# A streaming hybrid encoder step: the row factor of the conv columns is applied once, squared, and the group norm's epsilon takes over the rest

## The chip, the cores and the metric

The kernel runs on one core of one Trainium2 chip. The metric is the device time of one execution in microseconds (us). Engines are named as the profile names them: PE is TensorE (matmuls; PEld are its weight loads), DVE is VectorE, ACT is ScalarE, POOL is GpSimd, SP is SyncE, which issues most DMAs here.

## The reference

One layer works on 512 new prompt rows and 64 sample rows of width 2048, together 576 rows. Only the part around the change is shown; attention and the FFN are left out.

```python
hn = rmsnorm(x, g_norm1)              # x * R * g, with R = rsqrt(mean(x*x) + EPS), one R per row
proj = hn @ w_in                      # q, k, v for 8 heads; gb, gc, hc for 8 conv groups of 128 channels
u = gc * hc
conv = conv_w[0]*padded[:, 0:T] + conv_w[1]*padded[:, 1:T+1] + conv_w[2]*padded[:, 2:T+2]
o_conv = gb * conv
mix = concat([rmsnorm(o_attn, g_attn_out), rmsnorm(o_conv, g_conv_out)])
x = x + mix @ w_out
x = x + (silu(h2 @ w_gate) * (h2 @ w_up)) @ w_down      # h2 = rmsnorm(x, g_norm2)
```

`rmsnorm(o)` divides by `sqrt(mean(o*o) + EPS)`, with EPS = 1e-6. `u` is also an output (the last two rows are the conv state), `o_conv` is not.

## The kernel before

Activations lie transposed: channels on the 128 partitions, the 576 rows along the free dimension, in two halves of 288 (`HALVES`). Matrix products are made in fp32r with each operand split into a high and a low part, three matmuls per 128-deep step (`step`, L221 for plain products). The input is multiplied by the gain `g` only; the row factor R is left out of the matmul operands and is applied to the products. `R1` (128 x 576, the same on all partitions) holds it. `eps_r` (128 x 18), made early from the rows' mean squares by a small matmul, holds EPS * (mean(x*x) + EPS), that is EPS / R^2, with row 32b + p mod 32 at partition p, column b; the q and k norms use it.

Stages, in order: the input turned and projected; eight heads (`head`, `attend`); two conv groups by plain products (`conv_group`, STD = 2), while the last head's attention ends; six conv groups in pairs, as "units" `CU`, each a 2 x 2 block product with seven multiplications in place of eight (`conv_prepare` makes the weight operands on DVE and ACT, `conv_run` multiplies and evacuates); the attention rows' output projection, as "o" units of the same kind; the conv rows' output projection (`out_proj`); the FFN, again with seven products per block (L1582). `head_forms` is a generator that runs beside the second conv group: it norms the attention output and stores its block combinations to DRAM.

What sets the order: PE runs strictly in program order (`manual_schedule`). A `Pipeline` of generators interleaves side work with the matmuls: `pipe.tick()` once per three matmuls, and a generator's `yield n` puts its next part n ticks later. DVE, ACT, POOL and SP are ordered by a scheduler when the kernel is built, except where `manual_schedule` names them: SP during the heads and from the units on, and ACT and DVE from the last half of the second conv group to the ninth unit product (`start_mode`), where program order holds. Each engine works its queue in order.

The R factors before, for a conv group: `gc` is evacuated from PSUM times R1 (L960) and again times R1 (L961); `u` is that times `hc` straight from PSUM (L933, L935); `end_u` makes the taps (L941 on ACT, L943 twice on DVE); `gb` is evacuated times R1 (L975), multiplied by the taps (`put_o`, L950 and L952) and handed to `put_mix`, which scales, squares, splits and stores it (L549, L551). For a unit pair, `done` in `conv_run` adds a kept part (L1110) and multiplies every block by R1 (L1112): the two blocks i = 0, 1 of both columns c = 0 (`gc`) and c = 1 (`hc`) of a "u" unit, and all four blocks of a "b" unit (`gb` of two groups). `group_scale` sums the squares of `o_conv` by a matmul with ones and makes R_c = rsqrt(mean + EPS) with `rsqrt_mean` (L491 to L496); `out_proj` multiplies by R_c.

## Time and profile before

| | |
|---|---|
| time, median of 3 runs | 2362.01 us (2360.82 to 2364.43) |
| the profiled execution's own time | 2360.45 us |
| its span in the profile | 2358.7 us |
| PE busy | 2335.9 us, 99% of the span, 17551 matmuls |
| DVE busy | 1894.6 us, 80% |
| ACT busy | 1134.9 us, 48% |
| POOL busy | 300.3 us, 13% |
| mean granted TensorE clock | 0.999 |

All times inside the profile are counted from the start of the span; the profiled execution's own time is 1.75 us longer than its span. A timeline row gives start, duration, engine, line, operation, the tile written and the tiles read, and in brackets how long the engine sat idle before it and what released it. A row of a wait list gives who waited, for whom, and the total, the number and the longest of the waits. A row of a stretch ("windows") gives the busy time of each engine in it, the number of instructions, the granted TensorE clock, the DMA share and GB/s. The conv groups lie at about 396 to 485 us, the unit pairs at about 478 to 690 us.

### The profile page before, as it was taken

The page shows a single profiled execution, that of the slowest core. Times are in us where ns is not written, and L with a number is a line of the kernel's source. Part 1 is how long each engine was busy: PE and PEld are TensorE (multiplying, and loading weights), DVE is VectorE, ACT ScalarE, POOL GpSimd, SP SyncE. Part 2 cuts the span into 40 slices and gives each one's busy share as a digit, 9 for nine tenths or more (in the row PEclk, how much of TensorE's full clock was granted, in tenths as well). Part 3 has the DMA queues.
Part 4 walks back from the last instruction along what each step waited for, and adds up shares of the span by engine and source line. Part 5 has one row for each costly group of instructions (what it writes and reads, how often), then busy time and mean ns, then how long its engine had stood idle before and what let it go on. Part 6 is the DMA issues. An engine that isn't in the chain of part 4 may idle for free.

```text
span 2358.7 us, 43730 instructions
## 1 busy us (share of the span) xinstructions
PE 2335.9 (99%) x17551; PEld 2325.3 (99%) x17551; DVE 1894.6 (80%) x2828; ACT 1134.9 (48%) x1975; POOL 300.3 (13%) x401
## 2 busy tenths in 40 slices
PE   8999999999999999999999999999999999999998
PEld 8999999999999999999999999999999999999998
DVE  8666666788887899888888888888888777987896
ACT  6655555444445555444444444444444444444443
POOL 1111111422121220000000000000000002431222
PEclk9999999999999999999999999999999999999999
DMA  8565563773468555344344444444444936885554
GB/s 268 153 172 142 139 166 104 240 242 114 124 236 227 173 174 160 122 154 151 122 153 141 134 153 142 133 153 132 144 153 132 359 115 206 223 236 199 190 145 87
DMA packets 588996, 395.75 MB, mean 168 GB/s; under 512 B 100222, under 2 KB 577912, under 8 KB 588792
## 3 DMA queue, kind: packets, MB, share of 16 engines
q1 hardware_dynamic: 574968, 375.95, 51.2%
q0 software_dynamic: 8624, 16.22, 3.3%
q8 instruction: 137, 2.24, 0.4%
q10 hardware_dynamic: 5200, 0.79, 0.2%
q14 instruction: 67, 0.55, 0.1%
HBM read 301.46 MB, written 91.44 MB: 167 GB/s over the span
## 4 chain that ended last, share of the span: by engine, by line
PE 89%; DVE 5%; DMA 3%; issue 1%; ACT 1%; SPq 0%; POOL 0%; ACTq 0%; POOLq 0%; DVEq 0%
PE psy L1582 34%; PE psw L1582 17%; PE pj L221 13%; PE psx L1582 8%; PE psy L1086 6%; PE pjo L221 4%; PE psw L1086 3%; PE psx L1086 1%; DMA raw_a<-in_w_out_dram 1%; DVE whl L231 1%; PE po L794 1%; PE z L723 1%; DVE whl L1058 1%; DMA out_dram<-acc 0%; DVE x L375 0%
## 5 line engine op out<-in xcount | busy, mean ns | idle before, releaser
L1582 PE MATMUL psy<-h_s,whl 128*128 128x288 f32 x2787 | 413.5, 295 | 1.1 <-ACT part L1592 1.1
L221 PE MATMUL pj<-x,whi 128*128 128x288 f32 x1856 | 388.6, 298 | 0.2
L1582 PEld LDWEIGHTS psy<-h_s,whl 128*128 128x128 f32 x2787 | 384.8, 189 | 1.8 <-ACT part L1592 1.8
L231 DVE TENSOR_TENSOR whl<-raw_a,whl 128x1024 fp32r<-128x1024 f32 (+4 forms) x296 | 318.2, 1076 | 54.6 <-ACT whl L230 53.1
L1582 PE MATMUL psw<-t,whl 128*128 128x288 f32 x2400 | 347.0, 294 | 0.0
L1582 PEld LDWEIGHTS psw<-t,whl 128*128 128x128 f32 x2400 | 327.8, 188 | 0.0
L230 ACT CAST whl<-raw_a 128x1024 fp32r<-128x1024 f32 (+4 forms) x296 | 267.5, 906 | 113.1 <-issue 35.4
L221 PEld LDWEIGHTS pj<-x,whi 128*128 128x128 f32 x1856 | 303.6, 189 | 1.4 <-DVE x L375 0.7
L221 PE MATMUL pj<-x,wlo 128*128 128x288 f32 x928 | 274.3, 296 | 0.1
L231 DVE TENSOR_TENSOR whl<-raw_b,whl 128x1024 fp32r<-128x1024 f32 (+5 forms) x190 | 200.2, 1054 | 69.5 <-ACT whl L230 68.2
L230 ACT CAST whl<-raw_b 128x1024 fp32r<-128x1024 f32 (+5 forms) x190 | 164.9, 871 | 170.3 <-issue 73.5
L1592 ACT COPY part<-psy 128x288 f32<-128x288 f32 x242 | 96.4, 398 | 284.9 <-PE psy L1582 262.0
L1582 PE MATMUL psy<-t2t,whl 128*128 128x288 f32 x1212 | 183.0, 294 | 0.8 <-ACT part L1592 0.8
L1582 PE MATMUL psy<-b22m,whl 128*128 128x288 f32 x1212 | 183.3, 295 | 0.1
L221 PEld LDWEIGHTS pj<-x,wlo 128*128 128x128 f32 x928 | 174.7, 188 | 0.7 <-DVE wlo L442 0.3
L1582 PE MATMUL psx<-h_s,whl 128*128 128x288 f32 x1185 | 173.6, 294 | 0.0
L1582 PEld LDWEIGHTS psy<-t2t,whl 128*128 128x128 f32 x1212 | 167.8, 188 | 1.1 <-ACT part L1592 1.1
L1582 PEld LDWEIGHTS psy<-b22m,whl 128*128 128x128 f32 x1212 | 168.2, 188 | 0.4 <-ACT part L1592 0.4
L1582 PEld LDWEIGHTS psx<-h_s,whl 128*128 128x128 f32 x1185 | 162.4, 188 | 0.0
L1361 POOL DMA_DIRECT2D hid_dram<-form x3 | 2.2, 749 | 947.6 <-DVE form L231 947.6
L230 ACT CAST whl<-s 128x1024 fp32r<-128x1024 f32 (+5 forms) x81 | 72.2, 892 | 102.8 <-PE psw L1582 99.4
L1582 PE MATMUL psy<-t,whl 128*128 128x288 f32 x576 | 106.5, 294 | 0.0
(474 smaller groups left out, 4297.4 us busy)
## 6 DMA issues: line engine op xcount, KB each, us to landing
hid_dram<-form SPq DMA_DIRECT2D x147, 288.0 KB, 2.3
raw_a<-in_w_in_dram SPq DMA_DIRECT2D x41, 1024.0 KB, 5.8
raw_a<-in_w_gate_dram SPq DMA_DIRECT2D x22, 1024.0 KB, 5.7
raw_a<-in_w_up_dram SPq DMA_DIRECT2D x22, 1024.0 KB, 5.8
raw_b<-in_w_gate_dram SPq DMA_DIRECT2D x22, 1024.0 KB, 6.5
raw_b<-in_w_up_dram SPq DMA_DIRECT2D x22, 1024.0 KB, 6.6
h_s<-hid_dram SPq DMA_DIRECT2D x10, 2016.0 KB, 12.8
raw_a<-in_w_out_dram SPq DMA_DIRECT2D x16, 1024.0 KB, 6.4
```

The source lines that it names most:

```text
L221: mm(ps, w_[:, k, csl], x_, start=(k == 0 and n == 0), stop=(k == nk - 1 and n == 2))
L230: nc.scalar.copy(out=hi, in_=src)
L231: (lo_eng or nc.vector).tensor_tensor(out=lo, in0=src, in1=hi.bitcast(F32), op=ALU.subtract)
L723: mm(zb[i], a_[:, kk], b_[:, q0:TP], start=(n == 0), stop=False, skip_group_check=True)
L794: mm(po[:, i * P : 512], a_[:, i, :], b_[:, : 512 - i * P], stop=(i == 0 and n == 2), **kw)
L1058: tt(out=whl[:, 1], in0=src, in1=whl[:, 0].bitcast(F32), op=ALU.subtract)
L1086: mm(ps, whl[:, w_, j, :], x_, start=(start and j == 0 and q == 0), stop=(j == m - 1 and q == 2), skip_group_check=True)
L1361: q.dma_start(out=hid_dram[fp][2 * n - 2 : 2 * n].rearrange("f p t -> p f t"), in_=t.bitcast(F32))
L1582: mm(ps, whl[:, w_, j, :], x_, start=(start and j == 0 and q == 0), stop=(j == len(xs_) - 1 and q == 2), skip_group_check=True)
L1592: nc.scalar.copy(out=t, in_=st["y"])
```

## The change

R^2 goes onto `gc` alone, in one multiplication; `hc` and `gb` get no factor. So `u`, the taps and the conv state are what they were, and `o_conv` comes out divided by R. Its norm is the same if EPS is divided by R^2 as well, which is what `eps_r` holds for each row. `R1` is squared in place once (128 x 576), after the last head's values have been read with it. In `group_scale` the 18 columns of `eps_r` are spread on ACT, each over 32 columns of R_c, and turned in 32 x 32 blocks on DVE, so that column t of R_c holds the epsilon of row t; `rsqrt_mean` then adds this tile in place of the constant. Epsilon thus lies in R_c's own tile until R_c overwrites it.

```diff
+def rsqrt_mean(..., eps=None):
+        if eps is None: (as before)
+        else:
+            nc.vector.scalar_tensor_tensor(out=ms, in0=src, scalar=1.0 / n, in1=eps, op0=ALU.mult, op1=ALU.add)
...
 def group_scale(acc, dst, rows_of):
+        nc.scalar.copy(out=dst.rearrange("p (b c) -> p b c", c=32), in_=eps_r.unsqueeze(2).to_broadcast([P, NB, 32]))
+        nc.vector.transpose(out=dst, in_=dst)
...
-            rsqrt_mean(dst[:, a:b], ss, 8 * P, HALF, ms, t)
+            rsqrt_mean(dst[:, a:b], ss, 8 * P, HALF, ms, t, eps=dst[:, a:b])
...
-    def put_o(g, i, t):
+    def put_o(g, i, src, t):
-        nc.vector.tensor_tensor(out=t[:, : e - a], in0=t[:, : e - a], in1=c[:, a:e], op=ALU.mult)
+        nc.vector.tensor_tensor(out=t[:, : e - a], in0=src[:, : e - a], in1=c[:, a:e], op=ALU.mult)
...
         def evac_gc(ps, a, b):
             nc.vector.tensor_tensor(out=t, in0=ps, in1=R1[:, a:b], op=ALU.mult)
-            nc.vector.tensor_tensor(out=t, in0=t, in1=R1[:, a:b], op=ALU.mult)
...
         def evac_gb(ps, a, b):
-            nc.vector.tensor_tensor(out=t, in0=ps, in1=R1[:, a:b], op=ALU.mult)
-            put_o(g, a // HALF, t)
+            put_o(g, a // HALF, ps, t)
...
         def done(c, i, ps, part=None):                      # in conv_run
-            nc.vector.tensor_tensor(out=t, in0=ps, in1=R1[:, a:b], op=ALU.mult)
             if kind == "b":
-                put_o(g + c, i, t)
-            elif (1 - c, i) in st:
+                put_o(g + c, i, ps, t)
+                return
+            if c == 0:
+                nc.vector.tensor_tensor(out=t, in0=ps, in1=R1[:, a:b], op=ALU.mult)
+            else:
+                st[c, i] = ps
+            if (1 - c, i) in st:
...
+    nc.vector.tensor_tensor(out=R1, in0=R1, in1=R1, op=ALU.mult)      # ahead of the first conv group
```

More of the change, by code (lines that the diff above doesn't have):

```diff
@@ L484, in tile_hybrid_stream_step, with rsqrt_mean @@
     hpool.release()
-    def rsqrt_mean(dst, src, n, width, ms=None, t=None):
+    def rsqrt_mean(dst, src, n, width, ms=None, t=None, eps=None):
         if ms is None:
@@ L490, in rsqrt_mean @@
         y = tmp.tile([P, HALF], F32, tag="y", name="y")[:, :width]
-        nc.vector.tensor_scalar(out=ms, in0=src, scalar1=1.0 / n, scalar2=EPS, op0=ALU.mult, op1=ALU.add)
+        if eps is None:
+            nc.vector.tensor_scalar(out=ms, in0=src, scalar1=1.0 / n, scalar2=EPS, op0=ALU.mult, op1=ALU.add)
+        else:
+            nc.vector.scalar_tensor_tensor(out=ms, in0=src, scalar=1.0 / n, in1=eps, op0=ALU.mult, op1=ALU.add)
         nc.scalar.activation(out=y, in_=ms, func=AF.Ln)
@@ L944, in end_u @@
                                            op0=ALU.mult, op1=ALU.add)
-    def put_o(g, i, t):
+    def put_o(g, i, src, t):
         a, b = HALVES[i]
         c, e = taps(g), min(b, TP)
-        nc.vector.tensor_tensor(out=t[:, : e - a], in0=t[:, : e - a], in1=c[:, a:e], op=ALU.mult)
+        nc.vector.tensor_tensor(out=t[:, : e - a], in0=src[:, : e - a], in1=c[:, a:e], op=ALU.mult)
         if b > TP:
-            nc.vector.tensor_tensor(out=t[:, e - a :], in0=t[:, e - a :], in1=c[:, TP + 2 :], op=ALU.mult)
+            nc.vector.tensor_tensor(out=t[:, e - a :], in0=src[:, e - a :], in1=c[:, TP + 2 :], op=ALU.mult)
         put_mix(g, i, t, col("gc", g), bt["acc"][:, a:b], g == 0)
```

## The prediction

> **What bounds the kernel now.** I read the page's busy times first, then the waits of PE over the whole span, then PE's timeline around the waits that lie in the conv stage, then DVE's timeline behind each of them.

> ```profile
> PE 2335.9 (99%) x17551; PEld 2325.3 (99%) x17551; DVE 1894.6 (80%) x2828; ACT 1134.9 (48%) x1975; POOL 300.3 (13%) x401
> PE psx_s L352 <- DMA xsn<-in_x_sample_dram: 5.4, 1, 5.4
> PE psy L1086 <- DVE whl L1058: 1.8, 2, 1.0
> PE psx L1086 <- DVE cv L1110: 1.4, 1, 1.4
> PE ss L500 <- ACT sq L230: 1.4, 1, 1.4
> PE psw L1086 <- DVE whl L1058: 0.5, 1, 0.5
> PE psy L1086 <- ACT part L1095: 0.5, 2, 0.2
> ```

> PE is busy for 2335.9 of 2358.7 us, so all work of the other engines together can hold it up by 22.8 us, and 5.4 of that is the first load. The instruction order of the two kernels on PE is the same, row for row; the change takes no matmul away. So it can only win what PE waits for the conv evacuations: the L1086 rows, 1.8 + 1.4 + 0.5 us behind DVE and 0.5 behind ACT copies that aren't touched. The most that the change can save directly is 3.7 us, 0.16% of the time. I take 0.2%, 4.7 us, as what a measurement tells from no change.

> The four waits behind DVE all lie in one stretch, at the start of the unit pairs:

> ```profile
> 489.46 3.41 PE L1086 MATMUL psx<-x,whl 128*128 128x288 f32 x24 [1.45 <-DVE cv L1110]
> 493.46 3.31 PE L1086 MATMUL psw<-xs_t,whl 128*128 128x288 f32 x23 [0.46 <-DVE whl L1058]
> 510.33 3.34 PE L1086 MATMUL psy<-xs_t,whl 128*128 128x288 f32 x23 [0.73 <-DVE whl L1058]
> 518.01 3.21 PE L1086 MATMUL psy<-x,whl 128*128 128x288 f32 x22 [1.03 <-DVE whl L1058]
> ...
> 480.00:520.00 40.00, 36.30 (x266) 35.17 (x265) 33.62 (x41) 17.18 (x23) 7.96 (x11) 1.00 0.74 242
> 520.00:560.00 40.00, 40.00 (x305) 40.00 (x304) 37.12 (x49) 18.91 (x28) 11.97 (x14) 1.00 0.45 133
> ```

> Between 480 and 520 us PE is busy for 36.30 of 40; from 520 to 560 DVE is fuller still (37.12) and PE waits for nothing. Most of what the change removes lies there, beside matmuls that aren't late.

> **What it removes, and what that is worth.**

> ```profile
> L1112 DVE TENSOR_TENSOR cv<-cv,R 128x288 f32<-128x288 f32 x28 | 13.8, 496 | 0.5
> L1112 DVE TENSOR_TENSOR cv<-psy,R 128x288 f32<-128x288 f32 x8 | 3.6, 454 | 1.7 <-PE psy L1086 1.7
> L961 DVE TENSOR_TENSOR gcr<-gcr,R x4: 453/755/1055, 403.4 to 459.6; 128x288 f32<-128x288 f32 x4
> L975 DVE TENSOR_TENSOR gbr<-pj,R 128x288 f32<-128x288 f32 x4 | 1.8, 453 | 1.7 <-PE pj L221 1.7
> ```

> Of the 36 products of L1112, 12 stay (gc, two per "u" unit) and 24 go; the 4 of L961 and the 4 of L975 go. That is 24 x 0.48 + 4 x 0.755 (the middle of the shortest, median and longest shown) + 1.8 = 16.3 us of DVE time. It is worth something on the path only where DVE is late, so I follow the four waits.

> First wait (489.46). DVE's rows ahead of it:

> ```profile
> 483.40 1.23 DVE L1058 TENSOR_TENSOR whl<-raw_c,whl 128x1024 fp32r<-128x1024 f32 x1
> 484.54 0.45 DVE L975 TENSOR_TENSOR gbr<-pj,R 128x288 f32<-128x288 f32 x1
> 485.03 0.39 DVE L950 TENSOR_TENSOR gbr<-gbr,uc 128x224 f32<-128x224 f32 x1
> 485.34 0.22 DVE L952 TENSOR_TENSOR gbr<-gbr,uc 128x64 f32<-128x64 f32 x1
> ...
> 487.72 1.22 DVE L1058 TENSOR_TENSOR whl<-raw_c,whl 128x1024 fp32r<-128x1024 f32 x1 [1.05 <-ACT whl L1055]
> 488.87 0.45 DVE L1110 TENSOR_TENSOR cv<-psx,part 128x288 f32<-128x288 f32 x1
> ```

> PE waits for a PSUM bank that the last row frees. ACT, in order, first scales the gated half (after L952), squares it, copies a part and only then casts the weight that L1058 at 487.72 waits for. Without L975 the taps' product starts at 484.54 instead of 485.03, and all behind it comes 0.49 us earlier. **First term: 0.49 us.** The second wait (493.46) hangs on the same unbroken run of DVE work and moves with it: nothing more.

> Third and fourth wait:

> ```profile
> 504.48 0.46 DVE L1110 TENSOR_TENSOR cv<-psw,part 128x288 f32<-128x288 f32 x1 [3.20 <-POOL part L1141]
> 504.97 0.46 DVE L1112 TENSOR_TENSOR cv<-cv,R 128x288 f32<-128x288 f32 x1
> 505.39 1.23 DVE L1044 TENSOR_TENSOR raw_a<-raw_a,raw_c 128x1024 f32<-128x1024 f32 x1
> ...
> 509.05 1.23 DVE L1058 TENSOR_TENSOR whl<-cx,whl 128x1024 fp32r<-128x1024 f32 x1 [1.17 <-ACT whl L1055]
> ...
> 510.93 0.82 DVE L1112 TENSOR_TENSOR cv<-cv,R 128x288 f32<-128x288 f32 x2
> ```

> The row at 504.48 waits for a product of PE itself, so the chain hangs on PE and moves with it; from there L1112 at 504.97 (an hc block) goes, and L1044 starts 505.39 - 504.97 = 0.42 earlier. **Second term: 0.42 us** off the wait of 0.73. Of the two products at 510.93 one (hc) goes, half of 0.82: 0.4, and by the pitch of such rows 0.36. DVE runs without a break from there to the weight that PE waits for at 518.01. **Third term: 0.36 us** off the wait of 1.03. After that PE isn't late until 734 us, and what is late there (ACT copies) isn't touched.

> Sum: 0.49 + 0.42 + 0.36 = 1.27 us. The bounds of this sum are 0 (another wait takes over each time) and 3.7 (all four go).

> **What it adds and moves.** R1 squared (128x576, both operands in SBUF), the spread on ACT and the turn on DVE aren't in the trace. The nearest rows:

> ```profile
> L664 DVE TENSOR_TENSOR Ek<-Ek,r x8: 757/757/759, 54.2 to 387.0; 128x576 f32<-128x576 f32 x8
> 393.30 0.78 DVE L832 STREAM_TRANSPOSE Ev<-Ev 128x576 f32<-128x576 f32 x1
> 466.82 1.35 DVE L572 SCALAR_TENSOR_TENSOR o_ob<-o_ob,vec,acc_a 128x576 f32<-128x576 f32 x1
> 421.23 0.67 ACT L230 CAST sph<-sp 128x576 fp32r<-128x576 f32 x1 [4.16 <-PE po L794]
> ```

> The square takes 0.76 us at about 393 us, behind the last read of R1. None of PE's waits on DVE lies between 400 and 480 us, so it is hidden behind the last head's matmuls and costs nothing by itself. Its consequence is a matter of queues: the scheduler now puts the square and a weight's low part ahead of the turn of the last head's values, and on SP a 1 MB weight load ahead of the reload of these values. That load waits for DVE.

> ```profile
> 399.06 0.38 SPq L837 DMA_DIRECT2D vtok<-vt_dram  x1
> 402.41 0.38 SPq L185 DMA_DIRECT2D raw_a<-in_w_in_dram  x1
> raw_a<-in_w_in_dram SPq DMA_DIRECT2D x4, 1024.0 KB, 5.4
> L791 PE MATMUL po<-pr,vtok x2: 271/272/274, 419.1 to 419.2; 128*128 128x128 f32 x2
> ```

> So the values' load is issued at about 402.8 in place of 399.06 and lands, behind the weight's 5.4 us, at about 409 (estimate: 402.41 + 5.4, and 1 us for its own bytes). PE wants them at 419.1; ACT's cast and DVE's low part between are about half a us each. About 8 us of cover: cost 0. If it were gone, each us that they land after about 416 would be one us of PE.

> The spread and the turn stand, in the built kernel's instruction order, not late in the output projection but at about 467 us, into the generator that stores the attention output's forms, right behind the last L572, which frees the tile. The turn waits for ACT's spread; queued behind it on DVE are two products that free PSUM banks, the form casts and the weights' low parts. Price: 0.67 + 0.78 = 1.45 us if DVE had nothing else, and up to 0.67 + 1.35 = 2.02 (L572 at 466.82, an op of the same width in the same place). Ahead of it go two of the four L961, the long ones of 1.05 us, and one L975 of 0.49: 2.6 us. I take that these pay for it, so that the run ends at 483.40 as before; either end is kept: 1.1 us earlier (2.6 - 1.45, inside the bound of the first wait) or, where stores and POOL set that generator's pace, 2.0 later.

> The products of `put_o` now read PSUM. In the rows that costs nothing: L950 took 0.39 on 128x224 from SBUF (above), and from PSUM:

> ```profile
> 469.09 0.38 DVE L933 TENSOR_TENSOR uc<-pj,gcr 128x224 f32<-128x224 f32 x1
> ```

> [...]

> **The clock.**

> ```profile
> 884.00:886.00 2.00, 2.00 (x11) 2.00 (x12) 2.00 (x4) 0.89 (x2) 0.00 (x0) 0.67 0.99 321
> 886.00:888.00 2.00, 2.00 (x10) 2.00 (x9) 2.00 (x3) 1.05 (x1) 0.00 (x0) 0.50 1.09 392
> 486.00:492.00 6.00, 4.55 (x35) 4.35 (x34) 4.66 (x6) 2.66 (x6) 1.49 (x2) 1.00 1.03 299
> ```

> The wait of 1.4 us at L500 (883 us) was followed by a granted clock of 0.67 and 0.50: over these 4 us 21 matmuls ran, at full rate it would be 30, so about 1.2 us lost. The wait of 1.45 at 489 us left the clock at 1.00. So equal waits can trip it or not, and everything after 520 us now comes 1.3 us earlier. [...]

> **Rivals.**
> 1. The conv waits go almost wholly: the run before 483.40 ends 1.1 us earlier as well. Then 1.27 + 0.96 (what is left of the first wait) = 2.2 us: 2359.8. For it: DVE is busy throughout there. Against: ACT's form casts in that run wait for stores and POOL.
> 2. The clock isn't cut at 883 us any more (or is cut at one of the four waits): 1.2 us off, 2359.5, or 1.2 us on, 2361.9. Nothing in the profile decides it.
> 3. Slower: the spread and the turn at 467 us aren't paid for. The run ends 2.0 later, the first wait becomes 1.45 + 2.0 - 0.49 = 2.96 us, of which 2.0 - 1.27 = 0.7 us net stays; a wait twice as long as that at 883 us would trip the clock, 1.2 more: 1.9 us, 2363.9. It decides from the point where they delay that run by more than 1.27 us.
> 4. Slower by more: the values of the last head land 13 us later than I work out; 416 + 5 = 421 gives 5 us: 2367. Against it: a cover of 8 us.
> 5. The change doesn't do what it says: the instruction lists show DVE with 30 fewer (32 gone, the square and the turn added) and ACT with one more. Excluded.

> **How the numbers follow.** The profiled execution took 2360.45 us, span 2358.7; the sum makes it 2357.4 in the span. It lies 1.56 below the median of the runs shown, so against that median: 2362.01 - 1.27 = 2360.7. Chances: forecast 0.55; rival 1 0.15; rival 2 0.11; rival 3 0.13; rival 4 0.06. The runs before lay from 2360.82 to 2364.43, and as much spread is in any new median: all four waits gone is 2362.0 - 3.7 = 2358.3, less the 1.2 us by which the lowest run lies under the median 2357.1; above, rival 3 gives 2363.9, rounded up to 2364. More than 0.2% faster (below 2357.3) needs rivals 1 and 2 together and a good run: 0.05. Slower than 2366.7 is rival 4 and what I don't see: 0.07. Within: 0.88.

> **What would show it.** Right: PE's waits at L1086 behind DVE fall from 3.7 to about 2.4 us, with the first near 0.96, the third near 0.31, the fourth near 0.67; DVE busy falls by about 14.8 us (16.3 - 0.76 - 0.78) and PE's busy time stays. Rival 1: the wait at `psx` is under 0.4. Rival 3: it is over 2, with the turn ahead of it. Rival 4: a PE wait at `po` for ACT, DVE or a DMA. Wrong altogether: a new PE wait after 520 us, where orders haven't changed in kind, or matmuls that run slower with no wait.

## The result, and the profile after

The changed kernel takes 2364.98 us (median of 22 runs, 2363.2 to 2368.86) against 2362.07 us for the kernel before (22 runs beside them). The ratio is 1.0014, 95% interval 1.0008 to 1.0020: 2.9 us slower, 0.14%. That is within 0.2%, as the likeliest chance had it, but the time is 1 us above the range and the sign is the other one.

The profiled execution is the slowest of the 22: 2368.86 us, span 2367.0. First the page's busy line, then PE's waits over the whole span (who waited, for whom, us in total, times, longest):

```profile
PE 2339.2 (99%) x17551; PEld 2328.5 (98%) x17551; DVE 1879.2 (79%) x2798; ACT 1135.9 (48%) x1976; POOL 296.3 (13%) x401
```

```profile
PE ssg L503 <- ACT sqg L230: 3.3, 1, 3.3
...
PE psy L1089 <- ACT part L1098: 1.5, 2, 1.0
PE ss L503 <- ACT sq L230: 1.4, 1, 1.4
PE psx L358 <- DMA xin<-in_x_prompt_dram: 1.2, 1, 1.2
PE psy L1089 <- DVE whl L1061: 0.9, 2, 0.7
PE psx L1089 <- DVE cv L1113: 0.7, 1, 0.7
...
PE psw L1089 <- DVE whl L1061: 0.4, 1, 0.4
```

The waits that the prediction was about (L1089 behind DVE) did shrink, from 3.7 to 2.0 us. But the first row is new: PE waits 3.3 us at `ssg`, the sum of squares of the attention output's norm, for ACT's cast `sqg`. The kernel before has no wait there at all. What it costs is read from one row of the stretch 440 to 450 us, first before, then after (busy time and count of PE, PEld, DVE, ACT and POOL, then the granted clock, the DMA share and GB/s):

```profile
440.00:450.00 10.00, 10.00 (x78) 10.00 (x77) 9.60 (x16) 5.42 (x11) 3.38 (x4) 1.00 1.08 389
```

```profile
440.00:450.00 10.00, 6.60 (x37) 6.16 (x36) 3.94 (x9) 3.72 (x9) 0.00 (x0) 0.83 1.07 388
...
444.00:446.00 2.00, 1.27 (x7) 1.06 (x8) 0.99 (x3) 1.22 (x3) 0.00 (x0) 1.00 1.08 389
446.00:448.00 2.00, 2.00 (x11) 2.00 (x10) 1.27 (x4) 0.50 (x2) 0.00 (x0) 0.50 1.09 393
448.00:450.00 2.00, 2.00 (x12) 2.00 (x12) 1.45 (x3) 2.00 (x5) 0.00 (x0) 0.64 1.08 391
450.00:452.00 2.00, 2.00 (x17) 2.00 (x17) 2.00 (x5) 1.03 (x2) 0.64 (x1) 1.00 0.70 252
```

37 matmuls in place of 78: 41 fewer, at 10/78 = 0.128 us each 5.3 us. 3.3 of it is the wait; most of the other 2.0 is the clock, which was granted at 0.50 and 0.64 right behind the wait, so that 11 and 12 matmuls ran in 2 us where 17 run at full rate.

Why is the cast late? ACT's timeline of the changed kernel, then POOL's and SP's issues, then the tile `mx` over 425 to 460 us:

```profile
436.54 0.43 ACT L230 CAST sqg<-acc_a 128x288 fp32r<-128x288 f32 x1
...
444.15 0.43 ACT L230 CAST sqg<-acc_a 128x288 fp32r<-128x288 f32 x1 [6.83 <-DMA mix_dram<-mx]
```

```profile
437.09 0.96 POOL L556 DMA_DIRECT2D mix_dram<-mx  x1 [3.13 <-DVE mx L554]
```

```profile
436.41 2.67 SPq L917 DMA_DIRECT2D xs_t<-xs_dram  x2
```

```profile
DMA to landing us min/median/max: 2.7/4.8/7.0
```

ACT sat idle for 6.83 us until the DMA that stores `mx` (a half of the first conv group's output, 288 KB) had landed. Nothing in the arithmetic joins the two; they only share memory. `sqg` (`parts`) and `mx` (`put_mix`) come out of one pool tag, `hl`, with two buffers, and which buffer a tile gets is settled when the kernel is built; that it goes by the order in which the buffers come free is what the experiments below bear out. The store is issued at 437.09, beside two loads of 2304 KB issued at 436.41, and takes 7.0 us; the next one, without them, takes 2.7. The same cast in ACT's timeline of the kernel before:

```profile
436.69 0.43 ACT L230 CAST sqg<-acc_a 128x288 fp32r<-128x288 f32 x1 [2.02 <-PE ssg L501]
```

There the second cast got the buffer of the first one, which PE had read, and the following `mx` got the one whose store was in flight, when that had landed. The semaphores that the instructions wait for, which the traces keep, say it too: ACT's second `sqg` waits for PE and POOL in the kernel before, and for POOL's store queue, DVE and POOL in the changed one; the wait on the store queue has moved from the next `mx` to `sqg`.

The profiled run is 8.4 us longer than that of before, the medians differ by 2.9. Some of that is the start, in rows of before and after:

```profile
0.00:60.00 60.00, 51.66 (x370) 49.01 (x371) 47.61 (x105) 37.12 (x105) 10.39 (x24) 1.00 0.87 270
```

```profile
0.00:60.00 60.00, 49.59 (x346) 47.40 (x347) 47.26 (x105) 37.03 (x105) 10.49 (x24) 0.97 0.85 260
```

24 fewer matmuls in the first 60 us, about 3 us. Part of it is a later first load. But the row also has the clock at 0.97 in place of 1.00: it was cut behind a wait of 2.4 us, and this step started 14 matmuls where 26 start at full clock, about 1.6 us.

```profile
53.48:56.89 3.41, 3.29 (x14) 3.32 (x15) 3.27 (x8) 0.44 (x2) 0.15 (x1) 0.50 0.89 244
```

The code there is the same in what it does, and runs below show the start falling either way: in one_more_product and loads_later, which have the changed kernel's start, 370 and 374 matmuls fall in these 60 us, as in the kernel before (370). I don't count it to the change. Another 1.0 us is PE's wait for ACT's `part` in the output projection (1.5 against 0.5 us), which comes out between under 0.3 and 1.9 in the runs below. With 5.3 lost at `ssg` and 1.6 won at the conv waits that makes 7.7 of the 8.4.

### The profile page after: what moved, and what is told of

The parts are those of the page before. It is cut to its first block, busy times and chain, and to the rows that moved or that the text cites. A ratio compares the mean times of both kernels' runs of the same rounds, so it can differ in the third digit from the quotient of the medians.

```text
span 2367.0 us, 43702 instructions
## 1 busy us (share of the span) xinstructions
PE 2339.2 (99%) x17551; PEld 2328.5 (98%) x17551; DVE 1879.2 (79%) x2798; ACT 1135.9 (48%) x1976; POOL 296.3 (13%) x401
## 4 chain that ended last, share of the span: by engine, by line
PE 91%; DVE 4%; DMA 3%; issue 1%; ACT 1%; SPq 0%; POOL 0%; ACTq 0%; POOLq 0%; DVEq 0%
PE psy L1590 34%; PE psw L1590 17%; PE pj L221 13%; PE psx L1590 9%; PE psy L1089 6%; PE pjo L221 4%; PE psw L1089 3%; PE psx L1089 1%; DMA raw_a<-in_w_out_dram 1%; PE z L728 1%; PE po L799 1%; DVE x L375 0%; DVE whl L1061 0%; DVE whl L231 0%; DMA raw_a<-in_w_down_dram 0%
## 5 line engine op out<-in xcount | busy, mean ns | idle before, releaser
L221 PE MATMUL pj<-x,whi 128*128 128x288 f32 x1856 | 389.8, 298 | 0.3 <-DVE x L375 0.3
L230 ACT CAST whl<-raw_a 128x1024 fp32r<-128x1024 f32 (+4 forms) x296 | 267.8, 907 | 113.6 <-issue 35.4
L221 PEld LDWEIGHTS pj<-x,whi 128*128 128x128 f32 x1856 | 305.0, 190 | 1.1 <-DVE x L375 0.6
L221 PE MATMUL pj<-x,wlo 128*128 128x288 f32 x928 | 275.1, 296 | 0.1
L230 ACT CAST whl<-raw_b 128x1024 fp32r<-128x1024 f32 (+5 forms) x190 | 164.9, 872 | 170.8 <-issue 73.1
L221 PEld LDWEIGHTS pj<-x,wlo 128*128 128x128 f32 x928 | 175.5, 189 | 0.7 <-DVE wlo L442 0.3
L230 ACT CAST whl<-s 128x1024 fp32r<-128x1024 f32 (+5 forms) x81 | 72.3, 892 | 103.0 <-PE psw L1590 99.5
## 6 DMA issues: line engine op xcount, KB each, us to landing
raw_a<-in_w_in_dram SPq DMA_DIRECT2D x41, 1024.0 KB, 6.1
raw_a<-in_w_gate_dram SPq DMA_DIRECT2D x22, 1024.0 KB, 5.7
raw_a<-in_w_up_dram SPq DMA_DIRECT2D x22, 1024.0 KB, 5.9
raw_b<-in_w_gate_dram SPq DMA_DIRECT2D x22, 1024.0 KB, 6.5
raw_b<-in_w_up_dram SPq DMA_DIRECT2D x22, 1024.0 KB, 6.7
raw_a<-in_w_out_dram SPq DMA_DIRECT2D x16, 1024.0 KB, 7.2
```

Source lines behind the costliest of these rows:

```text
L221: mm(ps, w_[:, k, csl], x_, start=(k == 0 and n == 0), stop=(k == nk - 1 and n == 2))
L230: nc.scalar.copy(out=hi, in_=src)
```

## The experiments

The theories, as the expectations name them. **T**: the second `sqg` cast shares a buffer with a store in flight; the wait and the clock behind it lose about 5 us, the conv stage gains about 1.3. **U**: the spread and the turn of epsilon cost what is lost. **V**: the loss is the changed order of loads on SP, or the later waits. Each run below has 11 timed runs (one of 6) beside 15 to 33 of the kernel before.

**Own memory for the sums.** In `head_forms`, the sums take stage tiles instead of tiles of `hl`:

```diff
-        two = [parts("sqg") for _ in HALVES]
+        two = [(bt["stage"][:, NP - 1 - i, 0], bt["stage"][:, NP - 1 - i, 1]) for i in range(2)]
```

> The changed kernel, but the two tiles that hold the split sums of squares of the attention output (sqg in head_forms) are taken from the last two slots of the form staging tile, which is free at that time, and no longer from the pair of buffers that the conv halves' mx tiles use. Theory T (the changed kernel's loss is PE's wait at the second sum of squares, because that sum's tile became the one that the first conv half's store is still reading, plus the clock that is cut behind this wait): the wait of 3.3 us and the cut are gone, the time falls by 4 to 5.5 us against the changed kernel, and against the kernel before it is 0.5 to 2 us faster (my sum was 1.3). Theory U (the loss is the spread and the turn of the epsilon in the form generator): the time stays about 3 us above the kernel before. Theory V (the loss lies at the other queues moved, SP's reload of the last head's values, or in waits after 700 us): likewise about 3 above.

Measured: 2362.08 us, ratio 0.9999 (0.9990 to 1.0008); no wait at `ssg`. It is 2.9 us under the changed kernel, where 4 to 5.5 was expected, and level with the kernel before, where 0.5 to 2 us faster was. PE's timeline shows a wait at the first unit (the first row) that the changed kernel hasn't, and which I come back to below.

```profile
487.61 3.34 PE L1089 MATMUL psy<-x,whl 128*128 128x288 f32 x23 [0.86 <-DVE whl L1061]
491.91 3.44 PE L1089 MATMUL psx<-x,whl 128*128 128x288 f32 x24 [0.96 <-DVE cv L1113]
```

**The same edit on the kernel before**, as a control.

> The kernel before with own_sums' edit alone: the two split sums in the last slots of the form staging tile. It is the control for own_sums: if the edit is worth nothing by itself, it is within 0.7 us of the kernel before, and the difference to own_sums is what the change is worth without the tile (my sum: 1.3 us faster).

Measured: 2362.70 us, ratio 1.0001 (0.9992 to 1.0010). Memory of their own for the sums gains nothing where they didn't wait for a store. PE's timeline has a wait at the first unit here too, where the kernel before has none, so at least part of that wait comes with this edit:

```profile
485.32 3.34 PE L1086 MATMUL psy<-x,whl 128*128 128x288 f32 x23 [0.55 <-DVE whl L1058]
```

**One product more.** The changed kernel with one product that nobody uses, in the place of the removed one, in the first half of the first conv group only:

```diff
         def evac_gb(ps, a, b):
+            if a == 0 and g == 0:
+                nc.vector.tensor_tensor(out=t, in0=ps, in1=R1[:, a:b], op=ALU.mult)
             put_o(g, a // HALF, ps, t)
```

> The changed kernel with one more DVE instruction and nothing less: in the first half of the first conv group the product of gb with R is made as before, into the tile that the product with the taps then overwrites. In the built kernel this gives the tiles of the sums back to the order of the kernel before (the second sum reuses the first sum's tile, the second conv half waits for the store). Theory T: adding this instruction makes the kernel faster, by 4 to 5.5 us against the changed kernel, so 0 to 2 us faster than the kernel before; no wait over 0.5 us at the sums. Theories U and V: no faster than the changed kernel, about 3 us above the kernel before.

Measured: 2360.81 us, ratio 0.9993 (0.9984 to 1.0001). An instruction more, and 4.2 us less than the changed kernel: about half a microsecond of DVE work shifts the order in which the buffers come free, and the second `sqg` gets the first one's buffer again. No wait at `ssg`.

**The first half fused alone.** The other way round: the kernel before, with only that one product taken out (this half of `o_conv` then lacks its row factor).

```diff
-            nc.vector.tensor_tensor(out=t, in0=ps, in1=R1[:, a:b], op=ALU.mult)
-            put_o(g, a // HALF, t)
+            if g or a:
+                nc.vector.tensor_tensor(out=t, in0=ps, in1=R1[:, a:b], op=ALU.mult)
+            put_o(g, a // HALF, t, None if g or a else ps)
```

> The kernel before with a single DVE instruction taken away: in the first half of the first conv group gb is multiplied by the taps straight from PSUM, without the product with R (so this half of this group lacks its row factor; R isn't squared, the epsilon is the constant). In the built kernel this alone gives the second sum of squares the tile of the first conv half. Theory T: PE waits 3 to 3.5 us at that sum, the clock is cut behind it, and the time is 3.5 to 5 us above the kernel before although an instruction is gone. Any theory that blames the epsilon, the squared R or the other removed products: within 1 us of the kernel before.

Measured: 2365.69 us, ratio 1.0018 (1.0009 to 1.0027). Taking one instruction out costs 3.5 us, with the whole of the loss: PE's wait, then the stretch.

```profile
PE ssg L500 <- ACT sqg L230: 3.1, 1, 3.1
```

```profile
440.00:450.00 10.00, 7.64 (x44) 7.43 (x45) 6.59 (x13) 4.77 (x9) 0.74 (x1) 0.83 0.99 358
```

There is no spread, no turn, no squared R and no changed load in this kernel. U and V are not needed for the loss.

**The shared tile put into the kernel before.** No product is removed; the second half's sums are given the first `mx` tile by hand:

```diff
+            bt.setdefault("first", t)                         # in put_mix
...
-        two = [parts("sqg") for _ in HALVES]
+        two = [parts("sqg"), (bt["first"][:, 0], bt["first"][:, 1])]
```

> The kernel before, with one edit: the second sum of squares of the attention output is put into the tile of the first conv half, so that it waits for that half's store, as the changed kernel's tiles make it; all else is as before. Theory T: a PE wait of 3 to 4 us at the second sum and a cut clock behind it, the time 3.5 to 5.5 us above the kernel before. Theories U and V: within 1 us of the kernel before, since neither the epsilon nor the queues are changed.

Measured: 2366.42 us, ratio 1.0019 (1.0010 to 1.0028), 4.4 us slower. The wait list, then the stretch:

```profile
PE ssg L500 <- ACT mx L230: 3.2, 1, 3.2
```

```profile
440.00:450.00 10.00, 8.41 (x42) 8.21 (x43) 6.50 (x13) 4.75 (x9) 0.74 (x1) 0.66 0.89 322
```

The choice of buffer is enough by itself: same arithmetic, same instructions, and the loss is there.

**The loads later.** The loads of `xs_t` in a generator of their own, 30 ticks on, to see whether the store lands sooner without them.

```diff
-        for q in (1, 2):
-            load_sum(q)
+        def late_loads():
+            yield 30
+            for q in (1, 2):
+                load_sum(q)
+        pipe.spawn(late_loads())
```

> The changed kernel, but the two loads of 2.3 MB each (xs_t) that are issued as the form generator starts are issued 30 ticks (about 12 us) later. The second sum's tile still waits for the first conv half's store. Theory T, with the store late because it is queued beside 4.6 MB of loads (7.0 us to landing in the changed kernel, 2.7 for the next one): the store lands in 2 to 3 us, PE's wait at the second sum falls from 3.3 us to under 0.5, and the time is 0 to 2 us below the kernel before. If the store is slow by itself, the wait stays near 3 us and the time 3 above. Theories U and V: about 3 above.

Measured: 2366.51 us, ratio 1.0019 (1.0010 to 1.0027). The edit missed its aim: SP's order in that stretch is the scheduler's, and the loads were still issued ahead of the store (432.8 and 433.5 us). The wait of 3.0 us came again; on the store's time it says nothing.

**The loads behind the norm.** So they were tied to it by data: `load_sum` is called in `head_forms` behind the norm, and POOL first copies one column of the normed sum into the tile that is loaded.

```diff
+        for q in (1, 2):
+            load_sum(q, acc_a[:, T - 1 : T])                  # in head_forms
...
+        if behind is not None:
+            nc.gpsimd.tensor_copy(t[:, 0, 0, :1], behind)     # in load_sum
```

> The changed kernel, with the two loads of 2.3 MB (xs_t) made dependent on the finished norm of the attention output (one element of each tile is written from it first), so that they can't be issued before the first conv half's store has landed. The second sum's tile is still the one that this store reads. If the store is late only because it shares the DMA engines with these loads: it lands in 2 to 3 us (7.0 in the changed kernel), PE's wait at the second sum falls from 3.3 to under 0.5 us with no clock cut behind it, and the time is 3 to 5 us under the changed kernel, unless the later loads hold up the form stores, which would show as a longer wait at the start of the unit pairs. If the store is slow by itself: 6 to 7 us to landing and a wait of about 3 us, as in the changed kernel.

Measured: 2368.18 us (6 runs), ratio 1.0030 (1.0019 to 1.0042). The stores of `mx` in 425 to 480 us, then a cast in ACT's timeline, then PE's waits:

```profile
DMA to landing us min/median/max: 2.9/3.4/5.8
```

```profile
463.79 0.43 ACT L230 CAST hf<-o_oa 128x288 fp32r<-128x288 f32 x1 [5.33 <-DMA form_dram<-hf]
```

```profile
PE psx L1091 <- DVE cv L1115: 5.0, 1, 5.0
...
PE psy L1091 <- ACT whl L1060: 1.6, 1, 1.6
```

The first stores land in 2.9 and 3.4 us and PE doesn't wait at `ssg`: without the loads beside them the stores aren't late (7.0 us in the changed kernel). But the loads now run beside the stores of the attention forms: ACT's cast waits 5.33 us for one of these, and PE waits 5.0 us at the second product of the first unit. I take the one to follow from the other; no run tests it. At 6.0 us over the kernel before, this is worse than the changed kernel.

**Constant epsilon.** The kernel of own_sums without the spread and the turn and with EPS in place of EPS / R^2, so that only the cost of these two is taken out (`o_conv` is then normed with another epsilon).

```diff
-        nc.scalar.copy(out=dst.rearrange("p (b c) -> p b c", c=32), in_=eps_r.unsqueeze(2).to_broadcast([P, NB, 32]))
-        nc.vector.transpose(out=dst, in_=dst)
...
-            rsqrt_mean(dst[:, a:b], ss, 8 * P, HALF, ms, t, eps=dst[:, a:b])
+            rsqrt_mean(dst[:, a:b], ss, 8 * P, HALF, ms, t)
```

> own_sums (2362.08 us, the changed kernel with the sums in tiles of their own) without the spread and the turn: the conv norm adds the constant epsilon again, so the output differs from the reference's by that. Theory U (they delay the form generator and with it the first unit waits): 1 to 2 us faster than own_sums, with the first unit wait under 0.5 us instead of 1.0. My forecast (they are paid for by the removed products, or hidden): within 0.7 us of own_sums.

Measured: 2360.45 us, ratio 0.9991 (0.9982 to 1.0000). That is 1.6 us under own_sums, which is what theory U forecast (1 to 2) and not what I did (within 0.7); but the intervals of the two overlap, so the times alone don't settle it. In PE's timeline the wait of 0.86 at the first `psy` is 0.29 here:

```profile
485.85 3.34 PE L1087 MATMUL psy<-x,whl 128*128 128x288 f32 x23 [0.29 <-DVE whl L1059]
490.15 3.40 PE L1087 MATMUL psx<-x,whl 128*128 128x288 f32 x24 [0.95 <-DVE cv L1111]
```

So the spread and the turn make this wait 0.57 us longer, in this kernel. In one_more_product, which has them, the same wait is 0.31, and in the next kernel there is none. By PE's waits they cost between 0 and 0.6 us, then, by what else DVE has to do there; the other 1 us of the two times isn't explained. U is a small cost beside T, and not the loss.

**One tile for both halves.** What the experiments point to: the changed kernel with no choice left to the pool. The second half goes into the first half's tile, behind PE's sum.

```diff
-        two = [parts("sqg") for _ in HALVES]
-        for (sh, sl), (a, b) in zip(two, HALVES):
-            split(sh, sl, acc_a[:, a:b])
+        sh, sl = parts("sqg")
+        split(sh, sl, acc_a[:, :HALF])
         yield 6
-        for (sh, sl), (a, b) in zip(two, HALVES):
-            rsqrt_mean(acc_a[:, a:b], channel_sums(sh, sl, a, b, "ssg"), 8 * P, HALF)
+        for a, b in HALVES:
+            ss = channel_sums(sh, sl, a, b, "ssg")
+            if a == 0:
+                split(sh, sl, acc_a[:, HALF:])
+            rsqrt_mean(acc_a[:, a:b], ss, 8 * P, HALF)
             yield 4
```

> The changed kernel with the sums of squares of both halves of the attention norm through one and the same tile: the second half is split into it when the first half's sum has been read by PE. Nothing else is changed and no instruction is added. Theory T (the changed kernel loses because the second half's tile is the one whose store is still in flight): the second cast waits for PE's sum, done long before, PE no longer waits at ssg at about 444 us, the granted clock is 1.00 over 440 to 480 us, and the time is about 4 us under the changed kernel's: 2361 us, ratio 0.9995 (0.9985 to 1.0005). Conv waits as in one_more_product: near 0.3, 0.99, 0.43, 0.18, 0.69. Theories U (spread and turn) and V (the reload on SP): the time stays at about 2365, ratio 1.001.

Measured: 2360.47 us, ratio 0.9996 (0.9987 to 1.0005), 4.5 us under the changed kernel. ACT's cast, the stretch, and PE's four waits at the units:

```profile
436.36 0.43 ACT L230 CAST sqg<-acc_a 128x288 fp32r<-128x288 f32 x1 [2.36 <-PE ssg L503]
```

```profile
440.00:450.00 10.00, 10.00 (x78) 10.00 (x77) 9.25 (x15) 5.24 (x11) 3.57 (x5) 1.00 1.08 391
```

```profile
488.48 3.46 PE L1091 MATMUL psx<-x,whl 128*128 128x288 f32 x24 [0.94 <-DVE cv L1115]
492.48 3.31 PE L1091 MATMUL psw<-xs_t,whl 128*128 128x288 f32 x23 [0.42 <-DVE whl L1063]
508.93 3.33 PE L1091 MATMUL psy<-xs_t,whl 128*128 128x288 f32 x23 [0.32 <-DVE whl L1063]
516.24 9.65 PE L1091 MATMUL psy<-x,whl 128*128 128x288 f32 x71 [0.67 <-DVE whl L1063]
```

The cast waits for PE, 78 matmuls run in the stretch again, and the four waits are near those of the prediction (0.96, 0.46, 0.31, 0.67); the wait of about 0.3 us ahead of them, expected from one_more_product, isn't there. The interval includes 1: against the kernel before, this version can't be told from no change.

## Why the prediction was wrong

**The step that failed** is "None of PE's waits on DVE lies between 400 and 480 us, so it is hidden", with "Its consequence is a matter of queues". The part on what the change adds and moves followed instructions, queues and DMAs, and asked for each removed piece of DVE work only whether PE was waiting for it. It didn't ask which buffer each tile of a shared tag gets once that work is gone. One product of about 0.5 us less on DVE at about 430 us, off the path, changed that assignment, and the second `sqg` landed on a buffer with a store in flight. Price: 5.3 us in the stretch, by the count of matmuls. Both directions are shown: taking out that product alone brings the wait (first_half_fused), putting one in takes it away (one_more_product), and giving the buffer by hand in the kernel before brings it with nothing removed (before_shared_tile).

**The forecast sum held for these four waits.** In us, with what the prediction gave for each:

| | before | forecast | after | one_tile_twice |
|---|---|---|---|---|
| first | 1.45 | 0.96 | 0.73 | 0.94 |
| second | 0.46 | 0.46 | 0.43 | 0.42 |
| third | 0.73 | 0.31 | 0.18 | 0.32 |
| fourth | 1.03 | 0.67 | 0.70 | 0.67 |
| sum | 3.67 | 2.40 | 2.04 | 2.35 |

The changed kernel's four, from PE's timeline:

```profile
497.00 3.44 PE L1089 MATMUL psx<-x,whl 128*128 128x288 f32 x24 [0.73 <-DVE cv L1113]
501.01 3.35 PE L1089 MATMUL psw<-xs_t,whl 128*128 128x288 f32 x23 [0.43 <-DVE whl L1061]
517.36 3.30 PE L1089 MATMUL psy<-xs_t,whl 128*128 128x288 f32 x23 [0.18 <-DVE whl L1061]
524.67 1.60 PE L1089 MATMUL psy<-x,whl 128*128 128x288 f32 x10 [0.70 <-DVE whl L1061]
```

Gained: 1.63 us in the changed kernel, 1.32 in one_tile_twice, where 1.27 was forecast. Two things keep this from being a proof. In the changed kernel the first wait also fell because PE came later: in before_shared_tile, which removes nothing, it fell from 1.45 to 0.51 behind the same stall. And in own_sums and one_more_product a fifth wait stands ahead of the four (0.86 and 0.31), so that 0.55 and 1.07 us of gain are left.

The three repaired kernels take 2362.08, 2360.81 and 2360.47 us, and each interval includes no change. That the last lies so near the forecast 2360.7 is in part luck: its profile also lacks the clock cut at 883 us (rival 2 of the prediction) and has more wait there. A gain of 1.3 us is seen in PE's waits, not in the times. Rival 2 itself was priced too low: the half clock at 883 us costs about 1.6 us by the count below, since 35 matmuls and not 30 run in these 4 us at full rate. Rival 4's 13 us are 12 by its own figures (409 to 421); nothing hangs on that.

For the changed kernel the ledger is 5.3 - 1.6 = 3.7 us slower; measured 2.9, interval 1.9 to 4.7.

**The turn and the reload.** DVE's timeline has the turn, and SP's the reload:

```profile
474.39 0.77 DVE L602 STREAM_TRANSPOSE R_c<-R_c 128x576 f32<-128x576 f32 x1
...
492.58 0.38 DVE L955 TENSOR_TENSOR gbr<-pj,uc 128x224 f32<-128x224 f32 x1
```

```profile
405.55 0.39 SPq L185 DMA_DIRECT2D raw_a<-in_w_in_dram  x1
406.17 1.67 SPq L842 DMA_DIRECT2D vtok<-vt_dram  x1
```

The turn takes 0.77 us (priced 0.78). That removed work pays for it (rival 3's question) held but for 0 to 0.6 us, above. The values go behind a weight load, as worked out, and PE doesn't wait for them: rival 4 didn't happen. The product that now reads PSUM takes 0.38 us for 128x224 (the row at 492.58), and took 0.39 from SBUF in the kernel before, so the first term loses nothing by it. DVE's busy time fell by 1894.6 - 1879.2 = 15.4 us, forecast 14.8.

**The list of what would prove it wrong** named "a new PE wait after 520 us"; the new wait came at 444 us, in the stretch that had been set aside. The range came from the four waits and the rivals on them; nothing in it stood for a wait where there had been none.

## What to carry to other kernels

Where tiles share a pool tag, an edit off the critical path that changes when a buffer comes free can change which buffer the next tile gets; look in the instruction lists at what each user of that tag waits for, before and after, and above all for a wait on a store that has moved to another instruction. Here, with PE 99% busy, 1.6 us won at the conv waits were outweighed by one such wait of 3.3 us and the clock behind it, together 5.3. Give a tile on the critical path memory that no DMA reads, or fix by hand which buffer it reuses.

## What the runs showed of the hardware

A store of 288 KB on POOL's queue took 7.0 us to land beside two loads of 2304 KB (388 GB/s moved in the stretch); such stores between 425 and 460 us took 6.2 to 7.1 in the other kernels with loads beside them, and 2.7 to 3.4 without.

The length of a wait alone doesn't settle whether the clock is cut. It was cut to 0.50 behind waits of 3.30, 3.22, 3.07, 3.0 and 4.97 us, but in the kernel before also behind one of 1.37 (883 us). In one_tile_twice the same place has a longer wait and no cut; PE's timeline, then the stretches behind it:

```profile
883.14 0.40 PE L503 MATMUL ss<-sq,oner 128*128 128x288 f32 x1 [2.58 <-ACT sq L230]
```

```profile
884.00:886.00 2.00, 2.00 (x17) 2.00 (x16) 2.00 (x3) 0.87 (x2) 0.00 (x0) 1.00 0.95 263
886.00:888.00 2.00, 2.00 (x18) 2.00 (x16) 2.00 (x4) 1.39 (x2) 0.00 (x0) 1.00 1.08 392
```

Of the eleven profiles, five show the cut at this wait and six don't, with waits from 1.4 to 2.6 us. It is worth about 1.6 us, and so is part of what one profile differs from another.

By these counts a cut goes with few matmuls started within one step, and so with where the step's edge falls. Two steps of the kernel before, then two of one_tile_twice (the counts here include matmuls that began ahead of the step):

```profile
881.28:884.68 3.40, 1.86 (x12) 1.42 (x11) 3.23 (x8) 1.95 (x5) 0.00 (x0) 1.00 0.52 119
884.69:888.10 3.41, 3.41 (x17) 3.41 (x16) 3.41 (x5) 1.51 (x3) 0.00 (x0) 0.50 1.07 381
```

```profile
878.84:882.25 3.41, 1.72 (x13) 1.48 (x12) 2.22 (x6) 0.79 (x3) 0.00 (x0) 1.00 0.50 183
882.26:885.66 3.40, 2.42 (x16) 2.22 (x17) 3.30 (x7) 1.72 (x5) 0.00 (x0) 1.00 0.53 127
```

The wait of 1.37 us lies within one step, which started 11 matmuls, and the clock was cut. The wait of 2.58 is parted by an edge at 882.26 us: 11 and 16 started, and it wasn't. The steps before a cut weren't empty: all but two held some matmuls, and two held 11. At 11 the count alone doesn't tell. No run here moves an edge on purpose, and what cuts the clock isn't shown.
